# Later places for the last token tiles' transposes in the second feed-forward layer

## Chip, cores and metric

The kernel runs on one core of one Trainium2 chip. The metric is the device time of one execution in microseconds; the time of a kernel is the median of its runs. Three runs of the kernel before took 2224.02, 2228.5 and 2229.81 us.

## What is computed

Two residual blocks over 1024 tokens of width 1024, each followed by a feed-forward layer with a short causal convolution, and a final norm. Block 0 is a gated spatial and convolution mixer, block 1 a dilated attention. The part that matters here is the norm at the mouth of the second feed-forward layer and the up projection that reads it.

```python
def rms_norm(x, g):
    y = x * lax.rsqrt(jnp.mean(x * x, axis=-1, keepdims=True) + EPS)
    return y * g

def conv_ffn(x, norm_g, w_up, conv_w, conv_b, w_down):
    h = rms_norm(x, norm_g)
    u = causal_dwconv(h @ w_up, conv_w, conv_b)     # 3 taps
    gate, val = jnp.split(u, 2, axis=-1)            # 2 x 2816 channels
    return x + (jax.nn.silu(gate) * val) @ w_down

# for each layer i:  x = x + mixer_or_attention(x);  x = conv_ffn(x, ...)
# return rms_norm(x, final_norm_g)
```

## The kernel before

**Layout.** The 1024 tokens are eight tiles of 128 rows (`NT = 8`). Every fp32 product is made of three matmuls on operands split into a high and a low part (`mm3`, L257): high by high, low by high, high by low. The up projection needs the normed activations with channels on the partitions, so each normed token tile is transposed on TensorE: eight 128x128 transposes, into two PSUM banks named `psn`. Tiles 0 to 3 make the first half (512 tokens) of the operand, tiles 4 to 7 the second.

**Order.** The whole order is written by hand. A `Ticker` counts steps. A generator that issues matmuls yields after a small group, `drive` then ticks, and work filed with `after(n, f)` is issued n ticks later behind what has been issued by then. In the up projection's plain products (`up_units`) one step is six matmuls of 128x512. Each engine executes what it was given strictly in that order; semaphores make it wait for operands.

**The norm of one tile** (`norm_tile`, L343) is five pieces, filed from the tick at which the tile's residual sum is issued:

- `a`, one step later: ScalarE squares the row and sums it (L324).
- `mean`: VectorE makes the mean, GpSimd raises it to the power -1/2 (`sm`).
- `c`: three small VectorE operations refine the root; then the row is scaled. For tiles 0 to 5 (`i < NORM_POOL`) ScalarE scales (L337) and GpSimd multiplies with the gain; for tiles 6 and 7 VectorE does both in one `SCALAR_TENSOR_TENSOR` that writes `xn`.
- `d`, at step `4 + extra`: TensorE's eight transposes (L361) read `xn` and fill two `psn` banks.
- `e`, one step behind `d`: ScalarE copies both banks to `xr` (L370) and casts them to the high part `hTh` (L197); VectorE subtracts for the low part `hTl` (L129).

`extra` is 4 for tiles 0 to 5 and 2 for tiles 6 and 7. The caller (`norm_into`) adds 2 to it in the second feed-forward layer, but `norm_tile` uses that only for tiles 0 to 5.

**What runs around it.** The norm of the second feed-forward layer begins while the attention's output projection (`down_units`, `psd` banks) is still being issued; tile i is filed when its last product is. Then `ffn_up` follows. Two channel pairs are computed plainly, in four units with the first token half (24 matmuls each, bank `psu`), then four units with the second half. `Conv.put` takes each finished unit: ScalarE writes `y` with a scale and a bias (L954), VectorE adds two taps from the same bank (two `SCALAR_TENSOR_TENSOR` on `y`). The remaining 20 pairs are made with seven half-sized products in place of eight (`Pair`), which needs sums of the two token halves. `t_sums` makes them per tile pair (i, i+4): three VectorE operations `xr<-xr`, then one on GpSimd. It is filed three steps after tile i+4's `e` by the hook `as_they_come`. `t_parts` later splits the sums into the operands `t1` to `t4`. VectorE and GpSimd helpers record all their work as L129, so the trace tells them apart by tile names.

The residual rows `x` are also stored to DRAM (`x_ffn1`, L1700) as each tile's `f` runs; weights for the next pair (`wr`) are fetched by SyncE.

## Time and profile before

| | us |
|---|---|
| median of three runs | 2228.5 |
| lowest and highest run | 2224.02, 2229.81 |
| the profiled execution | 2224.66 |
| its span (first to last instruction) | 2223.0 |
| TensorE busy in the span | 2178.2 |
| VectorE busy | 1614.9 |
| ScalarE busy | 1098.0 |
| GpSimd busy | 705.2 |

The mean granted TensorE clock over the span is 0.996 of full speed. The page of the profile is read from its first part (busy time by engine) to the view of waits: TensorE is near full, so a change is worth what it takes out of, or puts into, the few places at which TensorE stands still. The stretch of this change lies at 1574 to 1600 us from the span's start.

### The profile page before, as it was taken

What the parts mean: (1) busy time and instruction counts of PE and PEld (TensorE: products, weight loads), DVE (VectorE), ACT (ScalarE), POOL (GpSimd) and SP (SyncE); (2) the same over time, 40 slices, a digit from 0 to 9 for tenths busy, and PEclk for the clock granted to TensorE, in tenths of its full rate; (3) what the DMA queues carried; (4) which work ended last, traced back from release to release, by engine and by line L of the source; (5) the groups of instructions that cost most, each with busy time, mean ns of one, the idle gap of its engine ahead of it and who ended that gap; (6) DMA issues with size and microseconds to landing.
All of it is one profiled execution on the core that took longest, in us unless ns stands there. A gap on an engine that the chain in (4) does not pass through costs nothing.

```text
span 2223.0 us, 29241 instructions
## 1 busy us (share of the span) xinstructions
PE 2178.2 (98%) x10448; PEld 1822.0 (82%) x10448; DVE 1614.9 (73%) x2576; ACT 1098.0 (49%) x1667; POOL 705.2 (32%) x540
## 2 busy tenths in 40 slices
PE   6999999999999999999999999999999999999998
PEld 6888788888888888878888888788788888888886
DVE  6998759877777765555777777876787777778556
ACT  5335365444444445254555555554554444444532
POOL 1122033766666330040000000112456666653001
PEclk9999999999999999999999999999999999999999
DMA  5478422344434597346343444723134444349943
GB/s 184 108 142 181 162 90 74 138 170 152 175 131 173 181 379 268 142 158 170 90 106 105 118 122 107 231 82 106 58 133 156 171 147 178 130 158 347 364 133 115
DMA packets 138834, 352.13 MB, mean 158 GB/s; under 512 B 16448, under 2 KB 16832, under 8 KB 138688
## 3 DMA queue, kind: packets, MB, share of 16 engines
q1 hardware_dynamic: 131920, 325.71, 43.6%
q0 software_dynamic: 5616, 20.36, 4.5%
q10 hardware_dynamic: 1152, 4.19, 0.5%
q8 instruction: 82, 1.34, 0.2%
q14 instruction: 64, 0.52, 0.1%
HBM read 216.01 MB, written 100.64 MB: 142 GB/s over the span
## 4 chain that ended last, share of the span: by engine, by line
PE 49%; DVE 2%; issue 2%; ACT 1%; DMA 1%; POOL 0%; SPq 0%; DVEq 0%; POOLq 0%; ACTq 0%
PE psd L1252 9%; PE psu L260 4%; PE psu L261 4%; PE psu L259 4%; PE po L1524 3%; PE psb L1076 3%; PE psb L1073 3%; PE psb L1074 3%; PE psc L1073 2%; PE psc L1076 2%; PE psc L1074 2%; PE pss L1437 2%; PE pss L1438 2%; PE ppt L1505 1%; PE ppt L1504 1%
## 5 line engine op out<-in xcount | busy, mean ns | idle before, releaser
L1252 PE MATMUL psd<-ab 128*128 128x512 f32 x1800 | 410.1, 389 | 0.0
L1252 PEld LDWEIGHTS psd<-ab 128*128 128x128 f32 x1800 | 337.5, 188 | 70.0
L259 PE MATMUL psu<-hTh,w 128*128 128x512 f32 (+1 forms) x592 | 237.0, 400 | 2.0 <-ACT hTh L197 2.0
L261 PE MATMUL psu<-hTh,w 128*128 128x512 f32 (+1 forms) x592 | 229.5, 388 | 0.0
L260 PE MATMUL psu<-hTl,w 128*128 128x512 f32 (+1 forms) x592 | 229.1, 387 | 0.2 <-DVE hTl L129 0.2
L197 ACT CAST ab<-ab 128x1024 fp32r<-128x1024 f32 x150 | 156.1, 1051 | 139.1 <-PE psd L1252 51.4
L129 DVE TENSOR_TENSOR ab<-ab,ab 128x1024 fp32r<-128x1024 f32 x150 | 192.0, 1334 | 32.9 <-ACT ab L197 32.3
L129 DVE TENSOR_TENSOR x<-psd,x 128x512 f32<-128x512 f32 x152 | 101.8, 687 | 136.4 <-PE psd L1252 109.8
L129 POOL MEMSET tt<- 128x256 f32 x64 | 19.9, 313 | 459.4 <-PE po L1524 266.0
L1110 ACT COPY sn<-psb 128x512 f32<-128x512 f32 x120 | 70.4, 587 | 171.1 <-PE psb L1076 128.4
L129 POOL TENSOR_TENSOR y<-y,y 128x512 f32<-128x512 f32 x66 | 94.9, 1438 | 182.5 <-DMA act<-y 151.9
L129 DVE TENSOR_TENSOR tt<-ppt,tt 128x512 fp32r<-128x512 f32 (+1 forms) x160 | 101.3, 634 | 45.9 <-ACT tt L197 44.9
L197 ACT CAST tt<-ppt 128x512 fp32r<-128x512 f32 (+1 forms) x160 | 86.7, 542 | 96.9 <-PE ppt L1505 87.2
L261 PEld LDWEIGHTS psu<-hTh,w 128*128 128x128 f32 x592 | 112.0, 189 | 23.2
L259 PEld LDWEIGHTS psu<-hTh,w 128*128 128x128 f32 x592 | 112.4, 190 | 19.0 <-ACT hTh L197 2.2
L260 PEld LDWEIGHTS psu<-hTl,w 128*128 128x128 f32 x592 | 112.6, 190 | 17.6 <-DVE hTl L129 0.5
L129 POOL TENSOR_TENSOR s<-wr 128x512 f32<-128x512 f32 x40 | 82.5, 2062 | 119.8 <-DVE psa L129 100.8
L129 DVE TENSOR_TENSOR wl<-wr,wh 128x1024 fp32r<-128x1024 f32 x88 | 119.3, 1356 | 0.0
L129 POOL TENSOR_TENSOR sm<-sm,mhalf 128x1 f32<-128x1 f32 (+2 forms) x38 | 31.2, 822 | 271.7 <-DVE sm L129 271.7
L1454 ACT ACTIVATE p<-p,sma 128x896 f32<-128x896 f32 (+7 forms) x128 | 99.6, 779 | 35.0 <-DVE sma L129 34.3
L1524 PE MATMUL po<-tt,v 128*128 128x256 f32 x640 | 108.7, 291 | 5.6 <-DVE tt L129 4.0
L129 DVE TENSOR_TENSOR pse<-psc,sn 128x512 f32<-128x512 f32 x40 | 28.0, 699 | 115.7 <-ACT sn L1110 115.7
(253 smaller groups left out, 5863.8 us busy)
## 6 DMA issues: line engine op xcount, KB each, us to landing
wr<-in_w_up_dram SPq DMA_DIRECT2D x88, 512.0 KB, 4.4
ab<-act SPq DMA_DIRECT2D x154, 256.0 KB, 5.4
act<-y SPq DMA_DIRECT2D x66, 512.0 KB, 2.9
wq<-in_w_down_dram SPq DMA_DIRECT2D x44, 512.0 KB, 5.3
wt<-wq SPq DMA_DIRECT2D x44, 512.0 KB, 4.6
ab<-wt SPq DMA_DIRECT2D x88, 256.0 KB, 5.4
ab<-in_w_down_dram SPq DMA_DIRECT2D x66, 256.0 KB, 5.8
wr<-in_w_qkv_dram SPq DMA_DIRECT2D x24, 512.0 KB, 3.7
```

The costliest lines, as they stand in the source:

```text
L129: return fn(*args, **kw)
L197: nc.scalar.copy(hi, src)
L259: nc.tensor.matmul(out_ap, st[0], mv[0], start=first, stop=False)
L260: nc.tensor.matmul(out_ap, st[0], mv[1], start=False, stop=False)
L261: nc.tensor.matmul(out_ap, st[1], mv[0], start=False, stop=last)
L1073: nc.tensor.matmul(ps, st[0], mv[0], start=f, stop=False, skip_group_check=True)
L1074: nc.tensor.matmul(ps, st[0], mv[1], start=False, stop=False, skip_group_check=True)
L1076: nc.tensor.matmul(ps, st[1], mv[0], start=False, stop=e, skip_group_check=True)
L1110: nc.scalar.copy(self.sn[key], self.b)
L1252: nc.tensor.matmul(ps, a[:, c], b[:, HALF:D], start=first and k == 0, stop=last and k == 2, skip_group_check=True)
L1454: nc.scalar.activation(p, p, AF.Exp, bias=sm[:, 2:3], scale=0.125, accum_out=lsum[hp][:, c:c + 1])
L1524: nc.tensor.matmul(po[:, c], v2[:, kb, :], tt[:, z, 256 * n:256 * n + 256], start=(g == 0 and n == 0 and z == 0), stop=(g == j and n == 1 ...
```

## The change

A table gives the number of added steps for each phase and tile. It is 0 for the first feed-forward layer and the attention's norm. In the second feed-forward layer it is 2 for tiles 0 to 6 and 4 for tile 7, and it now counts for tiles 6 and 7 too. Tiles 0 to 5 keep `extra = 6`; tile 6 goes from 2 to 4 and tile 7 from 2 to 6. Pieces `d` and `e` move together, and with `e` the hook's `t_sums`.

```diff
+NORM_MORE = {"ffn0": (0,) * NT, "attn": (0,) * NT, "ffn1": (2,) * 7 + (4,)}
...
     def norm_tile(i, x_t, gb, hT, on_pool, start=False, more=0):
...
-        extra = N_EXTRA + more if on_pool else N_EXTRA2
+        extra = (N_EXTRA if on_pool else N_EXTRA2) + more
...
-                norm_tile(i, xs[i], gb, hT, i < NORM_POOL, more=2 * (ph == "ffn1"))
+                norm_tile(i, xs[i], gb, hT, i < NORM_POOL, more=NORM_MORE[ph][i])
```

The added table shifts all later line numbers by one. The counts of instructions on every engine stay as they were, and the order on SyncE and GpSimd stays the same. Only TensorE, VectorE and ScalarE have rows in other places, all between the last products of the attention and the first second-half unit.

First place: TensorE in the first unit of the up projection (bank `psu_13794`). `xn_13702`, `xn_13752` and `xn_13811` are the normed rows of tiles 5, 6 and 7. Before:

```order
L261 MATMUL psu_13794<-hTh_13581,wl_13487 128x512
L361 MATMUL psn_13820<-ident,xn_13702 128x128 x4
L361 MATMUL psn_13825<-ident,xn_13702 128x128 x4
L361 MATMUL psn_13830<-ident,xn_13752 128x128 x4
L361 MATMUL psn_13835<-ident,xn_13752 128x128 x4
L259 MATMUL psu_13794<-hTh_13581,wh_13486 128x512
```

Tiles 5 and 6 were transposed back to back. In the changed kernel tile 5's eight transposes keep their place, and tile 6's stand in the second unit (bank `psu_13861`):

```order
L262 MATMUL psu_13794<-hTh_13581,wl_13487 128x512
L260 MATMUL psu_13861<-hTh_13577,wh_13507 128x512
L261 MATMUL psu_13861<-hTl_13578,wh_13507 128x512
L262 MATMUL psu_13861<-hTh_13577,wl_13508 128x512
L260 MATMUL psu_13861<-hTh_13577,wh_13507 128x512
L261 MATMUL psu_13861<-hTl_13578,wh_13507 128x512
L262 MATMUL psu_13861<-hTh_13577,wl_13508 128x512
L362 MATMUL psn_13868<-ident,xn_13752 128x128 x4
L362 MATMUL psn_13873<-ident,xn_13752 128x128 x4
L260 MATMUL psu_13861<-hTh_13577,wh_13507 128x512
```

Twelve matmuls now lie between the transposes of tiles 5 and 6: six that end the first unit and six of the second.

Second place: TensorE around tile 7's transposes. Before, they stood in the second unit (bank `psu_13878`), 24 matmuls behind those of tiles 5 and 6:

```order
L261 MATMUL psu_13878<-hTh_13581,wl_13508 128x512
L361 MATMUL psn_13898<-ident,xn_13811 128x128 x4
L361 MATMUL psn_13903<-ident,xn_13811 128x128 x4
L259 MATMUL psu_13878<-hTh_13581,wh_13507 128x512
L260 MATMUL psu_13878<-hTl_13582,wh_13507 128x512
```

In the changed kernel they stand in the third unit (bank `psu_13912`):

```order
L262 MATMUL psu_13912<-hTh_13581,wl_13809 128x512
L362 MATMUL psn_13939<-ident,xn_13811 128x128 x4
L362 MATMUL psn_13944<-ident,xn_13811 128x128 x4
L260 MATMUL psu_13912<-hTh_13581,wh_13808 128x512
L261 MATMUL psu_13912<-hTl_13582,wh_13808 128x512
```

Between tiles 6 and 7 there are now 36 matmuls, and from tile 7 to the first matmul of the second half 30, where before it were 54.

Third place: VectorE, from tile 5's low parts to those of tile 7. Before, the low parts of tiles 5 and 6 stood ahead of tile 7's root (`sm_13812`) and row (`xn_13811`):

```order
L129 TENSOR_TENSOR hTl_13782<-xr_13849,hTh_13781 128x4x128
L129 TENSOR_TENSOR hTl_13786<-xr_13849,hTh_13785 128x4x128
L129 TENSOR_TENSOR hTl_13782<-xr_13856,hTh_13781 128x4x128
L129 TENSOR_TENSOR hTl_13786<-xr_13856,hTh_13785 128x4x128
L129 SCALAR_TENSOR_TENSOR sm_13812<-sm_13812 128x1
L129 TENSOR_SCALAR sm_13812<-sm_13812 128x1
L129 TENSOR_TENSOR sm_13812<-sm_13812 128x1
L129 SCALAR_TENSOR_TENSOR xn_13811<-x_13270,sm_13812,gb_13435 128x1024
```

Tile 6's pair (`xr_13856` above, `xr_13885` below) has left this place: it now stands behind `wl_13847`, the low part of a weight, which follows the first unit's two taps. Tile 7's pair (`xr_13955`) stands here in the changed kernel, behind the second unit's two taps and the sums of tiles 2 and 6:

```order
L130 SCALAR_TENSOR_TENSOR y_13908<-psu_13861,fcw_13427,y_13908 128x511
L130 SCALAR_TENSOR_TENSOR y_13908<-psu_13861,fcw_13427,y_13908 128x510
L130 TENSOR_TENSOR xr_13678<-xr_13885,xr_13678 128x512
L130 TENSOR_TENSOR xr_13885<-xr_13885 128x512
L130 TENSOR_TENSOR xr_13885<-xr_13885,xr_13678 128x512
L130 TENSOR_TENSOR hTl_13782<-xr_13955,hTh_13781 128x4x128
L130 TENSOR_TENSOR hTl_13786<-xr_13955,hTh_13785 128x4x128
L130 SCALAR_TENSOR_TENSOR y_13962<-psu_13912,fcw_13427,y_13962 128x511
```

Before, the taps of the second unit stood behind tile 7's pair. So tile 7's row comes two operations earlier on VectorE, and its low parts come two operations (the second unit's taps) later.

## The prediction

> **What bounds the kernel now.** I read the page first, then TensorE's waits in the stretch of the change, then the timeline there, engine by engine.

> ```profile
> span 2223.0 us, 29241 instructions
> PE 2178.2 (98%) x10448; PEld 1822.0 (82%) x10448; DVE 1614.9 (73%) x2576; ACT 1098.0 (49%) x1667; POOL 705.2 (32%) x540
> PE psn L361 <- DVE xn L129: 3.4, 2, 2.0
> ```

> TensorE (PE) is busy for 98% of the span, so the kernel can only win what TensorE loses in waits or in clock. The third row is its only wait between 1535 and 1625 us: 3.4 us in two pieces, transposes waiting for VectorE's normed rows. They are those of tiles 6 and 7, as TensorE's timeline shows (start, duration, operation, idle time before it and what ended it):

> ```profile
> 1569.16 0.48 PE L259 MATMUL psd<-w,o 128*128 128x512 f32 x1
> ...
> 1573.79 0.40 PE L261 MATMUL psu<-hTh,wl 128*128 128x512 f32 x1
> 1574.03 1.04 PE L361 MATMUL psn<-ident,xn 128*128 128x128 f32 x8
> 1576.51 1.09 PE L361 MATMUL psn<-ident,xn 128*128 128x128 f32 x8 [1.45 <-DVE xn L129]
> 1577.36 0.48 PE L259 MATMUL psu<-hTh,wh 128*128 128x512 f32 x1
> 1577.67 0.39 PE L260 MATMUL psu<-hTl,wh 128*128 128x512 f32 x1
> ...
> 1578.83 0.39 PE L259 MATMUL psu<-hTh,wh 128*128 128x512 f32 x1
> ...
> 1582.69 0.39 PE L261 MATMUL psu<-hTh,wl 128*128 128x512 f32 x1
> 1585.04 1.62 PE L361 MATMUL psn<-ident,xn 128*128 128x128 f32 x8 [1.97 <-DVE xn L129]
> 1586.31 0.78 PE L259 MATMUL psu<-hTh,wh 128*128 128x512 f32 x1
> ...
> 1588.93 0.39 PE L259 MATMUL psu<-hTh,wh 128*128 128x512 f32 x1
> ...
> 1599.83 0.39 PE L259 MATMUL psu<-hTh,wh 128*128 128x512 f32 x1
> ```

> Matmuls overlap, so I count from start to start. The rows at 1574.03, 1576.51 and 1585.04 are the transposes of tiles 5, 6 and 7. The last row is the first matmul of the second half. Behind the second wait TensorE is slow for a while: six matmuls take from 1586.31 to 1588.93, where six behind tile 6 took from 1577.36 to 1578.83. The table of stretches gives the granted clock (the third number behind the colon of a row, after busy time and count):

> ```profile
> 1577.36:1582.00 4.64, 4.64 (x23) 1.00 0.57 177
> 1585.00:1586.31 1.31, 1.27 (x9) 0.65 0.43 44
> 1586.31:1588.93 2.62, 2.62 (x9) 0.52 0.52 184
> 1588.93:1592.00 3.07, 3.07 (x15) 1.00 0.00 0
> ```

> So the wait of 1.97 us is followed by a clock of 0.65 and 0.52, and the wait of 1.45 us by 1.00.

> **What leaves.** The undisturbed price of eight transposes is 0.79 us:

> ```profile
> 1568.37 1.03 PE L361 MATMUL psn<-ident,xn 128*128 128x128 f32 x8
> ```

> from this start to the matmul at 1569.16. Then:

> - Tile 6's transposes start 1576.51 − 1574.03 − 0.79 = 1.69 us late and take 1577.36 − 1576.51 = 0.85, which is 0.06 too long.
> - Tile 7's could start one matmul pitch (0.23 us, from 1573.79 to 1574.03) behind 1582.69, at 1582.92. They start 2.12 us late and take 1586.31 − 1585.04 = 1.27, 0.48 too long.
> - The six matmuls behind take 2.62 in place of 1578.83 − 1577.36 = 1.47: 1.15 too long.
> - Against this, one more change from transposes to matmuls is added, since tiles 5 and 6 no longer stand together. Its first pitch is 0.31 (1577.36 to 1577.67) and not 0.23: 0.1.

> If both waits go, TensorE gains 1.69 + 0.06 + 2.12 + 0.48 + 1.15 − 0.1 = 5.4 us.

> **Do both waits go?** From tile 5's start TensorE issues its eight transposes and twelve matmuls: 0.79 + 12 × 0.227 + 0.1 = 3.6 us (48 matmuls lie from 1588.93 to 1599.83: 0.227 us each). It reaches tile 6 at 1577.6. These are the VectorE rows that feed it, with two of GpSimd (POOL) and one of ScalarE (ACT):

> ```profile
> 1575.17 1.28 DVE L129 SCALAR_TENSOR_TENSOR xn<-x,sm,gb 128x1024 f32<-128x1024 f32 x1
> ...
> 1579.76 1.29 DVE L129 TENSOR_TENSOR hTl<-xr,hTh 128x512 fp32r<-128x512 f32 x2 [0.20 <-ACT hTh L197]
> 1581.77 1.29 DVE L129 TENSOR_TENSOR hTl<-xr,hTh 128x512 fp32r<-128x512 f32 x2 [0.72 <-ACT hTh L197]
> 1582.98 0.21 DVE L129 SCALAR_TENSOR_TENSOR sm<-sm 128x1 f32<-128x1 f32 x1
> ...
> 1583.61 1.28 DVE L129 SCALAR_TENSOR_TENSOR xn<-x,sm,gb 128x1024 f32<-128x1024 f32 x1
> 1584.81 0.69 DVE L129 TENSOR_TENSOR xr<-xr,xr 128x512 f32<-128x512 f32 x1
> ...
> 1586.87 1.53 DVE L129 SCALAR_TENSOR_TENSOR y<-psu,fcw,y 128x511 f32<-128x511 f32 x2
> 1588.31 1.22 DVE L129 TENSOR_TENSOR wl<-wr,wh 128x1024 fp32r<-128x1024 f32 x1
> 1589.44 0.68 DVE L129 TENSOR_TENSOR xr<-xr,xr 128x512 f32<-128x512 f32 x1
> ...
> 1592.21 1.67 DVE L129 TENSOR_TENSOR xr<-xr 128x512 f32<-128x512 f32 x1
> ...
> 1594.53 2.38 DVE L129 TENSOR_TENSOR hTl<-xr,hTh 128x512 fp32r<-128x512 f32 x2
> 1578.57 1.39 POOL L129 TENSOR_TENSOR sm<-sm,mhalf 128x1 f32<-128x1 f32 x1 [4.75 <-DVE sm L129]
> 1594.68 1.68 POOL L129 TENSOR_TENSOR xr<-xr,xr 128x512 f32<-128x512 f32 x1 [1.35 <-DVE xr L129]
> 1587.17 1.14 ACT L197 CAST hTh<-xr 128x512 fp32r<-128x512 f32 x2
> ```

> Tile 6's row is done at 1575.17 + 1.28 = 1576.45, 1.1 us before TensorE comes. Nothing that feeds it has moved. The first wait goes.

> Tile 7's root stands directly behind tile 5's low parts in the new order. A pair of low parts costs 1.21 (1581.77 to 1582.98), so the root starts at 1579.76 + 1.21 = 1580.97 in place of 1582.98; GpSimd's power, which it needs, is done at 1578.57 + 1.39 = 1579.96. The row follows 0.63 later (1582.98 to 1583.61) and is done at 1582.9. TensorE reaches tile 7 after eight transposes and 36 matmuls more, at 1577.6 + 0.79 + 36 × 0.227 + 0.1 = 1586.7. The second wait goes too, with 3.8 us to spare, and with it the slow clock.

> **What is late next.** The second half needs tile 7's low parts, and both sides have closed in: TensorE arrives sooner, and the low parts stand behind two more VectorE operations. TensorE comes to the first matmul of the second half at 1586.7 + 0.79 + 30 × 0.227 + 0.1 = 1594.4 (1599.83 before, so 5.4 earlier, the same sum as above), and to the second, which reads the low part, at 1594.6. VectorE from 1580.97: root 0.63, row 1.20 (1583.61 to 1584.81), sums of tiles 0 and 4 2.06 (1584.81 to 1586.87), two taps 1.44 (to 1588.31), weight's low part 1.13 (to 1589.44), tile 6's low parts 1.21, sums 2.06, the second unit's taps 1.44, sums 2.06. That is 13.2 us: tile 7's pair starts at 1594.2. Its first half takes 0.68 (the duration of its kin at 1589.44) and is done at 1594.9. **A new wait of 0.3 us.**

> Here lies the one price with two ends. VectorE operations with both inputs in SBUF and GpSimd's sums exclude each other: at 1592.21 an operation that costs 0.69 elsewhere took 1.67, and the pair at 1594.53 took 2.38 and not 1.29, while GpSimd's row at 1594.68 took 1.68. GpSimd's sum becomes ready at the same moment as tile 7's pair, now as before. If VectorE's first half goes first, the wait is 0.3; if GpSimd's sum does, it is 1.3 us more (1.68 less the 0.4 it stood), 1.6 in all. I take 0.3: before, the pair started at 1594.53, GpSimd at 1594.68. The second half-operand is read twelve matmuls (2.7 us) later and is done by 1596.9, in time. By either end the wait stays near the 1.45 us that left the clock alone. The other sums of GpSimd now fall beside the taps, which read PSUM, and slow nothing. The weight's low part for the fourth unit is done at 1587.4 and is read at 1589.4. ScalarE's copies and casts for tile 7 ended 1587.17 + 1.14 − 1585.04 = 3.3 us behind the start of its transposes; from 1586.7 that is 1590.0, before VectorE comes to them.

> **Does the gain last?** VectorE is then 5 us later against TensorE than it was. These rows tell whether it catches up before TensorE needs it:

> ```profile
> 1606.29 1.79 DVE L129 SCALAR_TENSOR_TENSOR y<-psu,fcw,y 128x1 f32<-128x1 f32 x4 [1.79 <-ACT y L954]
> ...
> 1611.15 1.49 DVE L129 TENSOR_TENSOR t1l<-xr,t1h 128x512 fp32r<-128x512 f32 x1 [0.71 <-ACT t1h L197]
> ...
> 1622.61 1.79 DVE L129 SCALAR_TENSOR_TENSOR y<-psu,fcw,y 128x1 f32<-128x1 f32 x4 [1.30 <-ACT y L954]
> ...
> 1627.30 0.70 DVE L129 TENSOR_TENSOR psa<-psa,sn 128x512 f32<-128x512 f32 x1 [0.57 <-PE psa L1076]
> 1636.00 0.50 PE L1076 MATMUL psb<-hTh,wl 128*128 128x512 f32 x1 [0.19 <-DVE wl L129]
> ```

> VectorE idles 1.79 + 0.71 + 1.30 + 0.57 = 4.4 us, each time for work that TensorE paces, and the second unit's taps (1.44) are already behind it. That is 5.8 us of room for 5.1 us of lead. At 1636.00 TensorE already waits 0.19 us for VectorE, so lag that is left would be paid there. I take 0.1 us; the ends are 0 and the whole 5.1. The fetches of weights and activations wait for TensorE or VectorE releases and move along.

> **Sum.** 5.4 − 0.3 − 0.1 = 5.0 us, 0.22%. The profiled execution took 2224.66 (its span and 1.7 us around it), so it would be 2219.7. That execution lies 3.8 us below the median of 2228.5; from the median the sum gives 2223.5. I forecast 2223. That is inside the 0.3% (6.7 us) that a measurement of this kernel tells from no change.

> **Rivals.**

> - *GpSimd goes first at tile 7's pair*, or VectorE is a microsecond later than my chain: gain 5.0 − 1.3 = 3.7, about 2225. For it: both start on one event. Against: the order at 1594.53 and 1594.68.
> - *Given back*: VectorE's lag reaches 1636 and TensorE waits there: gain 0 to 3, about 2227. For it: room and need are within 1 us, and the GpSimd sums of that stretch can block VectorE. Against: each idle piece ends on TensorE's own work.
> - *The slow clock stays*, if it has another cause than the wait: only 1.69 + 2.12 − 0.1 − 0.4 = 3.3 is won, about 2225. Against: the rows 1.00, 0.65 and 1.00 around the wait. [...]
> - *Slower*: tile 7's low part becomes a long wait with a slow clock behind it, at the first unit of the second half. A wait over 1.97 us would bring the slow clock's 0.48 + 1.15 = 1.6 as well, so the change loses from a wait of 3.8 us on, with the first half done at 1598.4 and not 1594.9. That takes three or more GpSimd sums (1.3 each) in VectorE's way; one or two in the way is what 1592.21 and 1594.53 show, and the new order takes the first of them away. At four sums (1.3 × 4 + 0.3 = 5.5 us) it would be 5.5 + 1.6 − 5.4 = 1.7 slower, about 2230.
> - *No effect*: that the order changes is seen in the rows; the waits would have to be something else than late rows, and they end on `xn` both times. I give it no share of its own.

> **Numbers.** Forecast (gain 4.5 to 5.4) 0.62; GpSimd first 0.14; given back 0.13; clock stays 0.05; slower 0.06. Three runs of before spread over 5.8 us, more than the whole gain, so the range takes the lowest run less 5.4 (2218.6) and, for the rivals, the median less nothing (2228.5): 2218 to 2229. Faster by over 0.3% needs 6.7 us, which the mechanism can't give; only the spread of the runs on top of the forecast reaches it: 0.22. Slower by over 0.3% needs the slower case and the spread: 0.04. Within: 0.74.

> **What would show it.** In the changed profile: no wait of `psn` for `xn` behind 1540 us, and a granted clock of 1.00 from 1570 to 1610; a new wait of `psu` L261 for `hTl` of about 0.3 us; the first matmul of the second half at about 1594.4, the span near 2218; VectorE idling less between 1600 and 1625, and a wait at `psb` L1077 of some tenths. A wait there of microseconds, a wait for `hTl` above 1.6, or a clock below 1.00 behind it would show my steps wrong.

## The result, and the profile after

| | before | after |
|---|---|---|
| median of 22 runs each, us | 2224.74 | 2223.13 |
| lowest and highest run | 2221.26, 2230.65 | 2218.30, 2224.67 |
| the profiled execution | 2224.66 | 2223.95 |
| its span | 2223.0 | 2222.2 |

The ratio of after to before is 0.9984 with an interval of 0.9978 to 0.9991: a gain of 3.6 us (2.0 to 4.9), where the prediction's sum said 5.0. It lies within the 0.3%. The two medians differ by less, 1.6 us, and the means of the 22 runs by 3.3 (2225.64 and 2222.34): the runs of before spread over 9.4 us with a long upper end, so the size of the gain is known to a microsecond or two only, and the traces have to say what it is made of.

The head of the page for the changed kernel reads almost as before:

```profile
span 2222.2 us, 29245 instructions
PE 2177.5 (98%) x10448; PEld 1820.8 (82%) x10448; DVE 1614.9 (73%) x2576; ACT 1097.5 (49%) x1667; POOL 704.6 (32%) x540
```

The spans differ by 0.8 us only. Tile 5's transposes, ahead of which nothing was moved, start at 1577.11 us and not at 1574.03; in all the traces of this study that start lies anywhere from 1571.2 to 1577.1. So I count from there. TensorE's timeline after (start, duration, operation, idle time before it and what ended it):

```profile
1577.11 1.04 PE L362 MATMUL psn<-ident,xn 128*128 128x128 f32 x8
1580.76 1.03 PE L362 MATMUL psn<-ident,xn 128*128 128x128 f32 x8
1589.81 1.04 PE L362 MATMUL psn<-ident,xn 128*128 128x128 f32 x8
1597.53 0.39 PE L260 MATMUL psu<-hTh,wh 128*128 128x512 f32 x1
1598.08 0.50 PE L261 MATMUL psu<-hTl,wh 128*128 128x512 f32 x1 [0.16 <-DVE hTl L130]
...
1619.75 0.39 PE L1074 MATMUL psb<-hTh,wh 128*128 128x512 f32 x1
...
1627.31 0.50 PE L1077 MATMUL psb<-t2h,wl 128*128 128x512 f32 x1 [1.50 <-DVE wl L130]
```

The transposes of tiles 6 and 7 (second and third row) no longer wait. The first matmul of the second half, fourth row, comes 20.42 us behind tile 5, where it took 1599.83 − 1574.03 = 25.80. The new wait for tile 7's `hTl` is there: the second matmul starts 0.55 behind the first and not 0.23, so 0.32 late. The last row is what the prediction put at some tenths, and at a later product: 1.50 us of waiting for `wl`, a low part of a weight.

The stretches around the transposes (start and end, length, busy time and count of TensorE, its weight loads, VectorE, ScalarE and GpSimd, then the granted clock) show no slow clock:

```profile
1580.00:1583.00 3.00, 3.00 (x18) 2.54 (x18) 1.59 (x4) 2.83 (x6) 1.34 (x1) 1.00 0.45 180
1583.00:1586.00 3.00, 3.00 (x15) 2.48 (x14) 2.90 (x7) 3.00 (x6) 0.05 (x1) 1.00 0.78 213
1589.00:1592.00 3.00, 3.00 (x19) 2.58 (x18) 3.00 (x5) 1.55 (x4) 0.40 (x1) 1.00 0.00 0
```

To see where the 1.50 us come from, first VectorE (DVE), GpSimd (POOL), ScalarE (ACT) and TensorE in the kernel before:

```profile
1603.21 1.28 DVE L129 TENSOR_TENSOR t2l<-xr,t2h 128x512 fp32r<-128x512 f32 x2
...
1607.99 2.44 DVE L129 TENSOR_TENSOR t2l<-xr,t2h 128x512 fp32r<-128x512 f32 x2
...
1625.52 1.22 DVE L129 TENSOR_TENSOR wl<-s,wh 128x1024 fp32r<-128x1024 f32 x1
1605.52 1.29 POOL L129 TENSOR_TENSOR s<-wr 128x512 f32<-128x512 f32 x1 [3.73 <-PE psu L261]
1625.70 3.44 POOL L129 TENSOR_TENSOR t4l<-xr,t4h 128x512 fp32r<-128x512 f32 x2 [13.61 <-ACT t4h L197]
1608.25 1.28 ACT L988 ACT_TABLE_LOAD   x1
1621.59 0.39 PE L1073 MATMUL psb<-hTh,wh 128*128 128x512 f32 x1
...
1627.49 0.39 PE L1076 MATMUL psb<-t2h,wl 128*128 128x512 f32 x1
```

and the same places after:

```profile
1597.34 2.38 DVE L130 TENSOR_TENSOR hTl<-xr,hTh 128x512 fp32r<-128x512 f32 x2
...
1604.58 3.52 DVE L130 TENSOR_TENSOR t2l<-xr,t2h 128x512 fp32r<-128x512 f32 x2
...
1609.71 1.94 DVE L130 TENSOR_TENSOR t2l<-xr,t2h 128x512 fp32r<-128x512 f32 x2
1612.77 0.69 DVE L130 TENSOR_TENSOR t1l<-xr,t1h 128x512 fp32r<-128x512 f32 x1 [1.12 <-ACT t1h L198]
...
1620.31 1.22 DVE L130 TENSOR_TENSOR y<-y,y 128x1024 f32<-128x1024 f32 x1
...
1624.94 2.32 DVE L130 TENSOR_TENSOR wl<-s,wh 128x1024 fp32r<-128x1024 f32 x1
1597.50 1.67 POOL L130 TENSOR_TENSOR xr<-xr,xr 128x512 f32<-128x512 f32 x1 [2.27 <-DVE xr L130]
1604.55 1.29 POOL L130 TENSOR_TENSOR s<-wr 128x512 f32<-128x512 f32 x1
1624.67 3.73 POOL L130 TENSOR_TENSOR t4l<-xr,t4h 128x512 fp32r<-128x512 f32 x2 [14.18 <-ACT t4h L198]
1609.87 1.28 ACT L989 ACT_TABLE_LOAD   x1 [3.48 <-DVE y L130]
...
1612.13 0.60 ACT L198 CAST t1h<-xr 128x512 fp32r<-128x512 f32 x1
```

`wl<-s` is the low part of a summed weight for the first pair made with seven products (`psb`). Its end, counted from tile 5's transposes, moved from 1626.74 − 1574.03 = 52.71 to 1627.26 − 1577.11 = 50.15 us: VectorE got 2.56 us earlier. TensorE got 4.92 earlier at that pair's first matmul (1621.59 − 1574.03 = 47.56, now 42.64). The matmul that first reads `wl` started 1627.49 − 1621.59 = 5.90 us behind that one before, 0.75 after `wl` was done. So it is now 4.92 − 2.56 − 0.75 = 1.61 us late; the trace shows 1.66 from start to start (1627.31 − 1619.75 − 5.90), 1.50 of it as idle time. VectorE stood still only once between 1597 and 1627, the 1.12 us in front of `t1l`. ScalarE's `t1h`, which ended that, stood behind the gate's SiLU (L989), and this had waited 3.48 us for VectorE's own taps.

### The profile page after: what moved, and what is told of

Read it like the earlier page. It is cut to its first block, busy times and chain, and to the rows that moved or that the text cites. A ratio compares the mean times of both kernels' runs of the same rounds, so it can differ in the third digit from the quotient of the medians.

```text
span 2222.2 us, 29245 instructions
## 1 busy us (share of the span) xinstructions
PE 2177.5 (98%) x10448; PEld 1820.8 (82%) x10448; DVE 1614.9 (73%) x2576; ACT 1097.5 (49%) x1667; POOL 704.6 (32%) x540
## 4 chain that ended last, share of the span: by engine, by line
PE 47%; DVE 3%; issue 2%; ACT 1%; DMA 1%; POOL 0%; SPq 0%; DVEq 0%; POOLq 0%; ACTq 0%
PE psd L1253 9%; PE psu L261 4%; PE psu L262 4%; PE psu L260 4%; PE psb L1077 3%; PE psb L1074 3%; PE po L1525 3%; PE psb L1075 3%; PE psc L1074 2%; PE psc L1075 2%; PE psc L1077 2%; PE ppt L1506 2%; PE pss L1438 1%; PE pss L1439 1%; PE ppt L1505 1%
## 5 line engine op out<-in xcount | busy, mean ns | idle before, releaser
L260 PE MATMUL psu<-hTh,w 128*128 128x512 f32 (+1 forms) x592 | 236.8, 400 | 1.9 <-ACT hTh L198 1.9
L261 PE MATMUL psu<-hTl,w 128*128 128x512 f32 (+1 forms) x592 | 229.1, 387 | 0.2 <-DVE hTl L130 0.2
L260 PEld LDWEIGHTS psu<-hTh,w 128*128 128x128 f32 x592 | 112.1, 189 | 19.2 <-ACT hTh L198 2.2
L261 PEld LDWEIGHTS psu<-hTl,w 128*128 128x128 f32 x592 | 112.4, 190 | 17.6 <-DVE hTl L130 0.5
```

What stands on the lines that cost most here:

```text
L260: nc.tensor.matmul(out_ap, st[0], mv[0], start=first, stop=False)
L261: nc.tensor.matmul(out_ap, st[0], mv[1], start=False, stop=False)
```

## The experiments

Two theories had to be tested. **The gain**: it is the two waits for `xn` with the slow clock behind the second. **The give-back**: VectorE has a backlog at `wl<-s`, partly because GpSimd runs beside it. The table has all profiled executions; "T5" is the start of tile 5's transposes, "pair" the first matmul of the first seven-product pair (`psb`). Spans are given to 0.1 us, so the last two of the three times are good to about 0.1. The lengthened waits and the second run of before were executed once each and are read by their traces alone.

| kernel | T5 to pair | pair to end | T5 to end | TensorE's waits from 1565 to 1660 us |
|---|---|---|---|---|
| before | 47.56 | 601.41 | 648.97 | xn 1.45, xn 1.97, psb 0.19 |
| after | 42.64 | 602.45 | 645.09 | hTl 0.16, psb 1.50 |
| tile 6 alone | 43.90 | 601.64 | 645.54 | xn 1.56, psb 0.64 |
| tile 7 alone | 44.32 | 601.41 | 645.73 | xn 1.43, hTl 0.27, psb 0.20 |
| both by two steps | 42.61 | 602.42 | 645.03 | psb 1.51 |
| t4 low parts later | 42.62 | 602.88 | 645.50 | hTl 0.18, psb 0.43, 0.47, 0.50 |
| gate products later | 42.63 | 601.25 | 643.88 | hTl 0.18 |
| low part earlier | 42.64 | 600.84 | 643.48 | none |
| both edits | 42.60 | 600.63 | 643.23 | none |
| gate products later, order of before | 47.57 | 600.59 | 648.16 | xn 1.44, xn 1.96 |
| lengthened wait | 45.28 | 601.40 | 646.68 | xn 2.94, psb 0.20 |
| lengthened wait, second time | 46.70 | 601.30 | 648.00 | xn 2.93, psb 0.19 |
| longer still | 49.05 | 601.37 | 650.42 | xn 4.31, psb 0.20 |
| before, second time | 47.51 | 601.41 | 648.92 | xn 1.42, xn 1.96, psb 0.20 |

### One part of the change alone

```diff
-"ffn1": (2,) * 7 + (4,)
+"ffn1": (2,) * 7 + (0,)      # tile 6 alone
+"ffn1": (2,) * 6 + (0, 4)    # tile 7 alone
+"ffn1": (2,) * 8             # both by two steps
```

> Only tile 6's transposes move (+2 steps), tile 7's stay on their old step. Measure: the stretch from the start of tile 5's transposes to the first matmul of the second half, 25.80 us before and 20.42 in the changed kernel. TensorE now comes to tile 7 some 7.2 us behind tile 5's start, and tile 7's row is done 8.9 us behind it (the changed kernel's trace), so the wait for xn stays, at 1.65 us. Theory (the wait itself slows the clock, somewhere between an idle time of 1.45 and 1.97): stretch 22.1 if 1.65 is still short enough, 23.7 with a clock near 0.5 behind it. Rival (the slow clock has another cause in that place): a slow clock although the wait is shorter than 1.97, or one in another place. Time: 1.7 to 3.3 us above the changed kernel.

> Only tile 7's transposes move (+4 steps), tile 6's stay behind tile 5's. Theory: the first wait stays at 1.45 us with a clock of 1.00 behind it, the second wait and the slow clock go: stretch 20.4 + 1.7 = 22.1 us. TensorE comes to the second half 1.7 us later than in the changed kernel, so no wait for hTl of tile 7, and the wait for the low part of the weight (1.50 in the changed kernel, psb L1077) falls to about 0: of the 1.7 most comes back there, time within 0.5 us of the changed kernel. Rival (the slow clock belongs to the place or to both waits together): a clock below 1.00 behind tile 6 or tile 7.

> Tiles 6 and 7 both move by two steps, tile 7's transposes stand twelve matmuls earlier than in the changed kernel, VectorE's and ScalarE's order is that of the changed kernel. Theory: tile 7's row is done 8.9 us behind tile 5's start and TensorE comes at 9.9, so no wait: stretch 20.4, wait for hTl 0.3, wait at psb 1.5, time as the changed kernel's within 0.5 us. Rival (the four steps are needed): a wait for xn at tile 7, stretch above 20.7.

Timed, they stand to before at 0.9994 (0.9985 to 1.0004), 0.9991 (0.9981 to 1.0001) and 0.9987 (0.9976 to 0.9998). The times alone leave open whether either single move gains anything; the traces tell more. Up to the pair, tile 6 alone brings 47.56 − 43.90 = 3.66 us, tile 7 alone 3.24, both 4.92. They don't add up, because tile 6's move alone shortens the wait for tile 7 and shows no slow clock either. TensorE's timeline and two stretches of the trace with tile 6 alone:

```profile
1584.73 1.06 PE L362 MATMUL psn<-ident,xn 128*128 128x128 f32 x8 [1.56 <-DVE xn L130]
```

```profile
1580.66:1584.08 3.42, 2.51 (x11) 1.70 (x10) 3.12 (x7) 3.42 (x7) 1.01 (x1) 1.00 0.52 176
1584.08:1587.49 3.41, 2.76 (x17) 2.45 (x18) 3.31 (x6) 3.41 (x8) 0.77 (x1) 1.00 0.41 145
```

Tile 7 still waits, 1.56 us, and the clock (behind the last bracket) stays at 1.00. The wait fell into two stretches here (0.91 and 0.65 us idle), which matters further down. The prediction's terms give 1.69 + 0.06 − 0.1 for tile 6, 1.97 − 1.56 for the shorter wait and 0.48 + 1.15 for the clock: 3.69, and 3.66 was measured. For tile 7 alone they give 2.12 + 0.48 + 1.15 − 0.3 (the wait for `hTl`) = 3.45, and 3.24 was measured; that wait, 0.27, was not in my expectation. Up to the end the single moves keep nearly all of what the change keeps (645.54 and 645.73 against 645.09): TensorE comes later to `wl`, so the wait there is 0.64 with tile 6 alone, and with tile 7 alone there is none at this product. Tile 7's two further steps in the change do nothing: with two steps for both the pair comes at 42.61, and the wait at `wl` is 1.51.

### What gives a part back

Three edits on top of later transposes; the second was also run on the order of before:

```diff
-                    after(2 + (4 * n + i) * 3 // 2, lambda i=i, m=m: t_parts(i, m))
+                    after(2 + (4 * n + i) * 3 // 2 + 3 * (l == 1 and m == 4), lambda i=i, m=m: t_parts(i, m))   # t4 low parts later
...
-                    after(6, self.gate)
+                    after(6 + (13, 8)[self.j] * (l == 1) if self.j < N_PLAIN else 6, self.gate)   # gate products later
...
-            after(lead + 1, s12_parts)
+            after(lead + 1 - 3 * (l == 1 and j == N_PLAIN), s12_parts)   # low part earlier
```

The first stands on the change as it is. "Gate products later" and "low part earlier" stand on both tiles by two steps.

> The changed kernel with the four splits into t4 issued three steps later in the second layer. In the changed kernel TensorE waits 1.50 us at psb L1077 for a weight's low part (wl<-s) that took 2.32 us on VectorE in place of 1.22, beside GpSimd's first t4l (started 0.27 us ahead of it). [...] Rival (VectorE is simply late by its backlog): the wait stays above 1.2.

> both_two with VectorE's two products y<-y,y of the two plain pairs issued 13 and 8 steps later in the second layer, into the place where VectorE idled 3.3 us behind the last wait. [...] Rival (what is late is paid elsewhere): a wait of over 1 us at a later psb, 645 us.

> both_two with the split of the same weight sum (wl<-s) three steps earlier for the first seven-product pair, so that VectorE makes this low part ahead of five other operations; VectorE's work is the same. Theory (backlog): the 1.51 us wait at this product goes, but the next low parts (wl<-wr) come as late as before and TensorE waits some 1 us there: from tile 5's transposes to the end 644.7 us or more. Rival (only the place of this one low part matters): no wait above 0.3, 643.6 us.

> The kernel before with the two products y<-y,y issued later as in gate_late; the transposes are not moved. Theory (VectorE's backlog costs only when TensorE comes early): the two waits for xn and the slow clock stay, the 0.19 us at psb L1076 go, from tile 5's transposes to the end 648.97 - 0.2 = 648.8 us, time as before within 1 us. Rival (the late products help by themselves): 648 us or less, time over 1 us below before.

With GpSimd's `t4l` out of the way, the wait for `wl` falls from 1.50 to 0.43, by 1.07 us: about the 2.32 − 1.22 = 1.10 that the row of `wl<-s` beside `t4l` was too long. The rival (above 1.2) falls. But the time comes back later. TensorE's timeline with the `t4` low parts later:

```profile
1626.01 0.50 PE L1077 MATMUL psb<-t2h,wl 128*128 128x512 f32 x1 [0.43 <-DVE wl L130]
1640.19 0.50 PE L1075 MATMUL psb<-t4l,wh 128*128 128x512 f32 x1 [0.47 <-POOL t4l L130]
1652.09 0.50 PE L1077 MATMUL psb<-t3h,wl 128*128 128x512 f32 x1 [0.50 <-DVE wl L130]
```

From T5 to the end it is no better than the change (645.50 against 645.09), and 0.9992 (0.9983 to 1.0002) in time.

Taking VectorE's work out of the way does help. With the gate products later, the `y<-y` that stood ahead of `wl<-s` goes behind it. VectorE's and GpSimd's timeline in that run:

```profile
1620.46 1.28 DVE L130 TENSOR_TENSOR t3l<-xr,t3h 128x512 fp32r<-128x512 f32 x2
1621.66 1.22 DVE L130 TENSOR_TENSOR wl<-s,wh 128x1024 fp32r<-128x1024 f32 x1
1621.78 7.00 POOL L130 TENSOR_TENSOR t4l<-xr,t4h 128x512 fp32r<-128x512 f32 x4 [14.18 <-ACT t4h L198]
```

`wl` now starts 0.12 ahead of `t4l` and takes 1.22; no `psb` waits any more, and T5 to end is 643.88 (ratio 0.9982, 0.9973 to 0.9991). Moving the one low part three steps forward gives 643.48 (0.9983, 0.9972 to 0.9994), again without a wait. There my expectation fell and its rival held: a backlog that is pushed aside should have come up at the next low part, 644.7 us or more, and it did not. So VectorE is not far behind everywhere; one deadline came too early for it.

On the order of before, the late gate products leave the two waits for `xn` and the slow clock, and the 0.19 at `psb` goes; the time is 0.9996 (0.9987 to 1.0006). But T5 to end is 648.16 against 648.97, a gain of 0.8 where I expected 0.2, close to the rival's 648 or less. Compared matmul by matmul, 0.5 of it comes at the product of that wait, 14 to 15 us behind the pair's first matmul, and 0.3 near 31 us, in delays too short for the list of waits. So the low parts are somewhat late in the order of before too, and the edit helps by itself; the 1.5 us at `wl<-s` appear only where TensorE comes early.

### A version with both edits

```diff
-"ffn1": (2,) * 7 + (4,)
+"ffn1": (2,) * 8
...
+                    after(6 + (13, 8)[self.j] * (l == 1) if self.j < N_PLAIN else 6, self.gate)
...
+            after(lead + 1 - 3 * (l == 1 and j == N_PLAIN), s12_parts)
```

> Tile 7 two steps later like tile 6, the gate products of the fourth and fifth unit 13 and 8 steps later (as in the run with late gate products), and the low part of the first seven-product unit three steps earlier (as in the run with that low part early). Theory: both edits remove one and the same wait of 1.50 us of psb for wl at 1627, so together they bring no more than either alone: from tile 5's transposes to the end 643.5 to 643.9 us (643.9 and 643.5 alone, 645.1 without them), no wait of psb over 0.3 us between 1600 and 1660, and a ratio to before of 0.998. Rival: the two moves collide on VectorE (the late gate products meet the other work of the later units), a wait of 0.5 us or more comes back, and the figure is 644.5 or more.

T5 to end 643.23: together they bring about what the better one brings (643.48), as they remove the same wait; it is 0.3 below the 643.5 to 643.9 that I expected. No wait is left between 1565 and 1660. Its median is 2220.6 us beside 2225.52 for before, a ratio of 0.9976 (0.9967 to 0.9985), the lowest ratio of this study: 5.3 us (3.3 to 7.3). That it beats the change itself rests on the traces (643.23 against 645.09); the two intervals overlap.

### What the slow clock hangs on

The prediction took a rule from one trace: a wait of 1.97 us slows the clock, one of 1.45 does not. To test it I lengthened the wait by moving tile 7's transposes one step, then two steps, the other way; tile 6's stay two steps later, so that only this wait is left:

```diff
-"ffn1": (2,) * 7 + (4,)
+"ffn1": (2,) * 7 + (-1,)     # lengthened wait
+"ffn1": (2,) * 7 + (-2,)     # longer still
```

> Tile 6's transposes move by +2 steps, tile 7's by -1, so that only one wait for xn is left and it is long: t6_only's 1.56 us plus one step (1.36), 2.9 us. Theory (a wait of about 2 us or more slows the clock, with no other wait near it): a granted clock well below 1.00 behind tile 7's transposes, six matmuls there in about 2.6 us and not 1.47, and from tile 5's transposes to the first seven-product pair 43.9 + 1.4 + 1.6 = 46.9 us. Rival (the slow clock of the kernel before came from both waits together): clock 1.00, 45.3 us.

The wait was 2.94 us, and the way to the pair took 45.28: the rival's figure, at a clock of 1.00. So length alone does not decide. All traces then showed a pattern: every slow stretch is one or two pieces of 3.41 us at a clock of 0.50, and within a run the pieces start at whole multiples of 3.413 us from one another, at another moment in each run. That gave a second theory, windows, for three more runs:

> The kernel before, unchanged, profiled a second time. Theory of windows: TensorE's granted clock is set in windows of 3.41 us that start at another moment in each run; a window with 1.84 us or more of idle TensorE makes the next one run at 0.50, one with 1.81 or less does not (from all slow stretches of the ten traces so far: each lasts 3.4 or 6.8 us, and within a run their starts lie whole multiples of 3.413 us apart). The wait of 1.97 us before tile 7's transposes can then be followed by 0.50 or by 1.00, about half of the time each: slow where at least 1.84 us of it lie in one window of the grid given by the slow stretch behind po's wait near 1433, and then 47.6 us from tile 5's transposes to the first seven-product matmul; otherwise 1.00 and 45.9 us. Rival (the wait, or the two waits together, slow the clock by themselves): 0.50 and 47.6 us wherever the grid lies.

> The kernel with the lengthened wait (tile 7's transposes one step earlier) profiled a second time; the first time its wait of 2.94 us left the clock at 1.00 and the way from tile 5's transposes to the first seven-product matmul took 45.3 us. Theory of windows: that wait lay with 1.14 and 1.81 us in two windows; the clock stays at 1.00 only where neither part reaches 1.84, which holds for 0.72 of the 3.41 us of positions, so about 1 time in 5. This time it is slow 4 times in 5, then for one window (or two): 47.0 us (or 48.7), and in any case as the grid from po's slow stretch says. Rival (a single wait doesn't slow the clock, it takes the two waits of before): 1.00 and 45.3 us again.

> Tile 7's transposes two steps earlier, directly behind tile 6's: the wait for xn grows from 2.94 to about 4.3 us. Theory of windows: wherever a wait of 4.3 us lies, at least 2.1 us of it fall into one window, so the clock is 0.50 behind it in every run, for one window at least: from tile 5's transposes to the first seven-product matmul 45.3 + 1.36 (six matmuls more behind the wait) + 1.7 = 48.3 us, 50.0 with two windows. Rival (a single wait doesn't slow the clock): 1.00 and 46.6 us.

The lines below are cut along each run's own grid, which I took from its slow stretch behind a wait of 3.27 us near 1433 (`po`, in the attention, the same in every kernel). The first busy time is TensorE's, so a row's length less it is TensorE's idle time. Before:

```profile
1431.80:1435.21 3.41, 1.39 (x6) 1.39 (x7) 3.35 (x5) 3.09 (x6) 3.41 (x2) 0.50 1.01 233
...
1581.99:1585.40 3.41, 1.45 (x9) 0.95 (x8) 3.31 (x7) 1.90 (x3) 0.00 (x0) 1.00 0.17 67
1585.40:1588.81 3.41, 3.41 (x13) 2.93 (x12) 3.31 (x6) 2.21 (x4) 1.29 (x1) 0.50 0.56 157
1588.81:1592.23 3.42, 3.42 (x16) 2.81 (x16) 3.32 (x6) 0.78 (x1) 0.57 (x1) 1.00 0.00 1
```

The whole 1.97 us lie in one window (3.41 − 1.45 = 1.96 idle), the next one runs at 0.50, and the one behind at 1.00. From 1431.80 to 1585.40 are 45 windows of 3.413. The lengthened wait, first time:

```profile
1575.68:1579.09 3.41, 2.28 (x15) 1.68 (x13) 2.71 (x5) 3.41 (x8) 1.40 (x1) 1.00 0.76 263
1579.09:1582.51 3.42, 1.60 (x11) 1.50 (x12) 3.27 (x6) 3.42 (x7) 0.00 (x0) 1.00 0.32 74
1582.51:1585.92 3.41, 3.41 (x16) 2.81 (x15) 3.38 (x6) 2.04 (x4) 1.30 (x1) 1.00 0.33 129
```

Its 2.94 us are cut by a boundary, 1.13 and 1.82 us idle, and nothing slows. The same kernel, second time:

```profile
1580.27:1583.69 3.42, 0.88 (x4) 0.38 (x2) 3.12 (x7) 3.42 (x6) 0.75 (x1) 1.00 0.52 153
1583.69:1587.10 3.41, 3.02 (x12) 2.76 (x12) 3.31 (x6) 2.86 (x7) 1.03 (x1) 0.50 0.51 151
```

One window holds 2.54 us of idle time, and the next runs at 0.50. The way to the pair is 46.70 and not 45.28 with the same program. The longest wait, 4.31 us:

```profile
1576.94:1580.35 3.41, 0.79 (x8) 0.55 (x6) 2.83 (x6) 3.41 (x8) 1.40 (x1) 1.00 0.83 261
1580.35:1583.77 3.42, 1.73 (x9) 1.76 (x9) 3.28 (x6) 3.12 (x6) 0.00 (x0) 0.50 0.32 90
1583.77:1587.18 3.41, 3.41 (x9) 2.65 (x9) 3.38 (x6) 1.62 (x3) 1.29 (x1) 0.50 0.30 109
```

Two slow windows, and 49.05, between the 48.3 and 50.0 expected for one and two, since a part of the first fell into the wait. The rival (a single wait is harmless, it takes the two of before) falls with these two runs.

Two things stay open. First, how often a run of before meets the slow clock at tile 7. The second profile of before has it again (1.96 us idle in one window, then 0.50, 47.51 to the pair), and so has the order of before with late gate products: three of three, where a random position would, by my estimate with 1.84 us, give about half. In all three the wait lay whole inside a window, so they don't speak against windows, but a trace of before with the clock at 1.00 was not met. Second, the bound. My 1.81 and 1.84 us were too sharp: in the second lengthened run a window near 977 with 3.42 − 1.56 = 1.86 idle left the clock alone, while windows with 1.69 (tile 7 alone) and 1.61 (both by two steps) near 980 slowed it. Cutting all fourteen traces by their grids from 50 to 2200 us shows how far the bound can be told. Of the windows at full clock, all 32 with 1.90 us or more of idle time were followed by 0.50, and all with 1.51 or less by 1.00; between 1.61 and 1.86 four were followed by 0.50 and six by 1.00. Behind windows that themselves ran at 0.50 less was enough: eight with 0.93 us or more of idle time were followed by another slow one, those with 0.55 or less never. What decides between 1.61 and 1.86, these runs don't settle.

## Why the prediction was right, and where it was wrong

**What leaves: right.** 5.4 us were predicted between tile 5 and the second half, 25.80 − 20.42 = 5.38 were found. Tiles 6 and 7 come 3.65 and 12.70 us behind tile 5; the prediction had 3.6 and 12.7. The single terms hold too, by the runs with one tile moved.

**The new wait: right.** 0.3 was predicted, 0.32 measured, and the order on which it rested came true: tile 7's pair started at 1597.34, GpSimd's sum at 1597.50, and the pair took 2.38 again. The rival "GpSimd first" did not happen. GpSimd's sums beside the taps slowed nothing, as predicted: those at 1588.10 and 1593.94 took 1.29 us each, and the pairs of taps beside them 1.53 each, where the pair at 1599.64, with no GpSimd work beside it, took 1.52.

**The slow clock: the outcome right, its rule incomplete.** The clock is 1.00 from 1569 to 1660. But "the wait of 1.97 us is followed by 0.65 and 0.52, the wait of 1.45 by 1.00" was read as a matter of length. What the traces show is how much of a wait fell into one window: 1.96 us in one was followed by 0.50, and 2.94 us cut into 1.13 and 1.82 by 1.00. The threshold that the rival "slower" used, "a wait over 1.97 us would bring the slow clock", therefore does not hold: 2.94 us brought it once of two times. The 1.63 us of this term were won in the profiled pair; an estimate from the windows is that a run of before in which the wait falls across a boundary would not have them to lose; none was met.

**Does the gain last: this step failed.** It took 0.1 us (bounds 0 and 5.1) and looked for it at 1636. The pair-to-end column says 602.45 − 601.41 = 1.0, and the wait is at the first seven-product pair, 1627 after. The delay there is larger, 1.7 to 1.8 us from start to start; 0.6 of it comes back at the two places, 14 to 15 and 31 us behind the pair's first matmul, at which before lost time itself. Two things were wrong in "5.8 us of room for 5.1 us of lead":

- *The deadline was taken too late.* One idle piece in the room, the 0.57 at 1627.30, lies behind `wl<-s`, which I had not looked for.
- *The idle time and the durations were taken as fixed.* VectorE still stood 1.12 us for ScalarE's `t1h`. The prediction took each idle piece as paced by TensorE; this one hangs on VectorE's own taps by way of ScalarE, so it moves along with VectorE. And moving VectorE against GpSimd changed what collides: the `t2l` pair went from 1.28 to 3.52 us as GpSimd's `s<-wr` at 1604.55 and the sum behind it now run beside it, and `wl<-s` from 1.22 to 2.32 beside `t4l`; two others got 0.50 and 0.80 shorter. So 5.8 − 0.57 − 1.12 − 2.24 − 1.10 + 0.50 + 0.80 = 2.1 us of room was left, about the 2.56 by which VectorE did move. Against TensorE's 4.92, the 2.56 and the 0.75 that `wl` had to spare leave 1.6 missing.

The mechanism, and that GpSimd can block VectorE in that stretch, stood among the rivals as "given back", with a gain of 0 to 3; the truth lies between it and the forecast, outside the 4.5 to 5.4 that was given a chance of 0.62. The rival "GpSimd first" named 3.7, close to what came, but for a cause that did not occur. What the rows show of the collision: `t4l` began 0.27 us ahead of `wl` and `wl` took 2.32; with the gate products later `wl` began 0.12 ahead and took 1.22.

**The sum and the number.** 5.0 us were predicted; the traces give 648.97 − 645.09 = 3.9, the times 3.6 (2.0 to 4.9). That the forecast of 2223 is met by a median of 2223.13 is partly chance: I took the gain off a median of three runs, 2228.5, while 22 runs have 2224.74. A base 3.8 us too high and a gain too large (5.0, where the medians differ by 1.6 and the ratio gives 3.6) worked against each other. The profiled execution of before, 2224.66, was the better base, and the sum from it would have been 2219.7. Both lie in the range.

## What to carry to other kernels

When a wait on the busiest engine is removed, list every later operand for which that engine will now come early, and compare each one's slack with the lead; the first short one sets what is kept, and here it was found only behind the change. Count an engine's idle time as room only up to that deadline, and only the part that the sped-up engine paces, not a piece that comes back to the lagging engine's own work through another; reckon with VectorE operations getting slower where the move puts them beside GpSimd's (here `wl<-s` from 1.22 to 2.32 us, and the `t2l` pair from 1.28 to 3.52). If the new deadline is the only short one, moving that one operation earlier, or other work behind it, recovers what was given back (1.2 to 1.9 us here, some of it from delays that before had too).
